# Differential attention: the score products of two heads issued as one group

## The chip, the cores and the metric

The kernel runs on one core of a Trainium2 chip. Its time is the device time of one launch in microseconds (us). Three runs of the kernel before gave 1320.67, 1320.77 and 1320.94 us, so the median is 1320.77 us. Beside the runs there is one profiled execution, from which every duration below is taken.

The engines have short names. PE is TensorE, the matrix engine, and PEld is its weight load, which runs beside the matmuls. DVE is VectorE, ACT is ScalarE, POOL is GpSimd and SP is SyncE, which issues nearly all transfers here. Every engine works through its own queue in order.

## The reference, cut to what matters

The program is a two-layer block for 256 tokens plus 16 learned "meta" tokens, with 1024 features. Each layer has a mixer with three branches (retention, a gated recurrence called hgrn2, and differential attention), a gated sum of the branches, and a feed-forward part with a short convolution. The change touches only the differential attention:

```python
q = rope(q.reshape(b, l, 2 * DA_HEADS, DA_DH), pos).reshape(b, l, DA_HEADS, 2, DA_DH) * DA_DH ** -0.5
k = rope(k.reshape(b, l, 2 * DA_HEADS, DA_DH), pos).reshape(b, l, DA_HEADS, 2, DA_DH)
...
s = jnp.einsum('bqhmd,bkhmd->bhmqk', qb, k)
p = jax.nn.softmax(jnp.where(allowed, s, MASK_VALUE), axis=-1)
w = p[:, :, 0] - lam * p[:, :, 1]
return jnp.einsum('bhqk,bkhe->bqhe', w, v)
...
o = _rms(o) * subln_g.astype(F32) * (1.0 - lambda_init)
```

There are 8 heads. Each head has two maps (m = 0 and 1) of 64 features each. Both maps give a causal softmax over the keys, the second is taken from the first with a learned factor, and the difference weighs 128-wide values. The result of a head is normalised over its 128 features.

## The kernel before, in words

**The main stream.** All dense layers are products of 128 x 128 weight tiles with 272 columns of tokens (258 in the second layer). Each is done as three products of rounded parts (weights high and low, tokens high and low): lines L890, L891 and L892. The weights arrive from memory in chunks of eight tiles (`wraw`, 512 KB). ACT rounds a chunk (`whi`, L575) and DVE makes the remainder (`wlo`, L575). Line L575 is a helper that records every ACT, DVE, POOL and small PE operation, so such operations are told apart by the names of their tiles.

**The rest.** The branches' own small products, softmaxes and norms are placed between main products. No engine has a fixed loop: the program first records every operation with an estimated cost, a key (the time when it should run) and its data, and a planner then simulates the engines and writes out one order for each queue. An operation is not placed more than 12 us (`EARLY`) ahead of its key. An operation that is ready and whose key is overdue goes ahead of a main product. The planner also counts buffers: an operation that opens a new tile is placed only when a buffer of that ring is free in the simulation. The function `behind` records a job (a list of operations), and `settle` spreads the keys of the jobs that end at one mark over the time up to that mark. With `apart` = 2, the first operation of a job waits for the end of the job two places before it: the third head of a block waits for the end of the first.

**The attention.** The heads come in two blocks of four, `+daa` and `+dab`, in each of the two layers, so 16 heads in all. A block is a job `da_first` (the 16 meta queries of its four heads), four jobs `da_head`, and a job `da_tail` (the last 16 tokens). Its result, `da`, is split into rounded parts `b2hi` and `b2lo`, which are the token operands of the main products named `b2`.

**One head.** `da_head` does this, with the names of the tiles:

1. POOL copies 16 columns into `a1` (tag `wts`).
2. PE forms the scores in one recorded operation, `scores` (line L1316): two tiles of keys (272 and 144 wide) times two maps, four calls. A call in 32-bit floats becomes two instructions, so a head has a group of 8. A map takes 64 of the 128 rows of the array. The results go to two banks of PSUM, tag `bank` (name `ds`).
3. DVE adds the mask and takes the row maximum, four times (to `two_a` and `two_b`).
4. ACT exponentiates four times. DVE forms the reciprocals and combines the two maps, in six more instructions.
5. PE transposes three 128 x 128 pieces into `wt` (tag `bank`), ACT copies them to `a1`, POOL copies the tails to `dt`.
6. PE multiplies with the values into `do` (tag `acc`), four instructions.
7. ACT copies two small pieces to `dot`. `sub_norm` squares (`hsq`), rounds (`hsh`, `hsl`), averages on PE (`ms`, tag `bank`), takes the inverse root on ACT (`hr`) and writes `da` on DVE, reading `do` once more.

PSUM has eight banks: four for the main products (two pairs, tag `main`), two with tag `bank` and two with tag `acc`. The tags `wts`, `two_a`, `two_b` and `dm` have two buffers each.

Of the kernel before, what the change touches and what calls it, by code (L numbers as in the profile page):

```python
# [37 lines left out]
TAIL = T - 2 * P  # L38
# [189 lines left out]
C_COS_R, C_SIN_R, C_COS_D, C_SIN_D, C_MASK, C_IDENT, C_OWN, C_DECT, C_FIRST, C_SUM, C_MAP, C_END = \  # L228
# [405 lines left out]
def _trace(ctx, tc, plan, a, depth, probe):  # L634
    nc = tc.nc
    act = _Engine(plan, nc.scalar, "act", 0.094, 0.833e-3)
# [33 lines left out]
    def temp(cols, tag, bufs=2):  # L670
        return new(tp, [P, cols], F32, tag, bufs, tag)
# [16 lines left out]
    def ts(out, x, s1, s2, op0, op1=ALU.bypass):  # L688
        dve.tensor_scalar(out=out, in0=x, scalar1=s1, scalar2=s2, op0=op0, op1=op1)
# [275 lines left out]
    for li in range(depth):  # L965
# [330 lines left out]
            act.activation(st[f"dw{b}"], wt[:, : 4 * META], AF.Copy)  # L1296
            st[f"dt{b}"], st[f"do{b}"] = (temp(P, n, 1).rearrange("p (g h t) -> p g h t", g=2, h=4) for n in ("dt", "dot"))

        def da_head(b, hd):
            q, k, vt, out = st[f"dq{b}"], st[f"dk{b}"], st[f"dvt{b}"], st[f"da{b}"]  # L1300
            scale = DA_DH ** -0.5

            a1 = temp(T + P + TAIL, "wts")
            pool.tensor_copy(a1[:, :META], st[f"dw{b}"][:, hd * META : (hd + 1) * META])
            tiles = ((META + P, T, 0), (META, META + P, T))
            sb = [temp(2 * T, tag) for tag in ("two_a", "two_b")]
            ss = [bank("ds") for _ in range(2)]
            red = temp(12, "dm")
            nm, sm, cf = (red[:, 4 * i : 4 * i + 4].rearrange("p (t m) -> p t m", m=2) for i in range(3))


            def scores():
                for q0, nk, at in tiles:
                    for m in range(2):
                        half = slice(64 * m, 64 * m + 64)
                        nc.tensor.matmul(ss[m][:, at : at + nk], q[half, hd, q0 : q0 + P], k[half, hd, :nk], start=True, stop=True)  # L1316

            plan.add("pe", scores, 0.95, [x[:, : T + P + META] for x in ss], [q[:, hd, :], k[:, hd, :]])
            plan.hold(*sb, a1)
            for i, (q0, nk, at) in enumerate(tiles):  # L1320
                mask = const[:, C_MASK + T - nk : C_MASK + T]
                for m in range(2):
                    cols = slice(at, at + nk)
                    dve.tensor_tensor_reduce(out=sb[m][:, cols], in0=ss[m][:, cols], in1=mask, scale=1.0,
                                             scalar=-3e38, op0=ADD, op1=ALU.max, accum_out=nm[:, i, m : m + 1])
            ts(nm, nm, -scale, None, MUL)
            for i, (q0, nk, at) in enumerate(tiles):
                for m in range(2):
                    p = sb[m][:, at : at + nk]
                    act.activation(p, p, AF.Exp, bias=nm[:, i, m : m + 1], scale=scale, accum_out=sm[:, i, m : m + 1])  # L1330
            dve.reciprocal(cf, sm)
            tt(cf[:, :, 1], cf[:, :, 1], nlam[:, li : li + 1].to_broadcast([P, 2]), MUL)
            for i, (q0, nk, at) in enumerate(tiles):
                p0, p1 = (x[:, at : at + nk] for x in sb)
                ts(p1, p1, cf[:, i, 1:2], None, MUL)
                stt(p0, p0, cf[:, i, 0:1], p1, MUL, ADD)
            w = sb[0]
            wt = bank("wt")
            pe.transpose(wt[:, :P], w[:, :P], ident)
            pe.transpose(wt[:, P : 2 * P], w[:, P : 2 * P], ident)  # L1340
            pe.transpose(wt[:, 2 * P : 3 * P], w[:, T : T + P], ident)
            act.activation(a1[:, META + P : T + P], wt[:, : 2 * P], AF.Copy)
            act.activation(a1[:, META : META + P], wt[:, 2 * P : 3 * P], AF.Copy)

            for g, c in ((0, 2 * P), (1, T + P)):
                pool.tensor_copy(st[f"dt{b}"][:, g, hd, :], w[:, c : c + TAIL])
            o = acc_bank("do")
            ec = slice(hd * P, hd * P + P)
            pe.matmul(o[:, t0:T], vt[:, 0, ec], a1[:, t0:T], start=True, stop=False)
            pe.matmul(o[:, P + META : T], vt[:, 1, ec], a1[:, T : T + P], start=False, stop=True)  # L1350
            for g, c in ((0, 2 * P), (1, P)):
                act.activation(st[f"do{b}"][:, g, hd, :], o[:, c : c + TAIL], AF.Copy)
            sub_norm(out[:, hd, t0 : 2 * P], o[:, t0 : 2 * P])
# [302 lines left out]
```

## Time and profile before

| | before |
|---|---|
| median of three runs | 1320.77 us |
| the profiled execution, its own time | 1320.99 us |
| its span, first to last instruction | 1319.2 us |
| PE, busy share of the span | 99% |
| DVE, ACT, POOL, busy share | 74%, 64%, 6% |
| granted clock of TensorE | 0.999 of full speed |
| score groups of 8 instructions (`ds`, L1316) | 16, first at 285.9 us, last at 1051.9 us |

The profile page gives the busy time of each engine, the chain of work that ended last, and the costliest groups of instructions. The start of one PE instruction to the start of the next is the useful measure on PE, because matmuls overlap in the pipeline: a main product is listed as 0.29 us long, while the next one starts after 0.12 us. In the timelines a row shows the start, the length, the engine, the line, the operation and the names of the tiles, and x8 means that eight instructions of one kind are merged into the row. A wait is put down to the operation that ended last before the waiting one could start.

### The profile page before, as it was taken

What the parts mean: (1) busy time and instruction counts of PE and PEld (TensorE: products, weight loads), DVE (VectorE), ACT (ScalarE), POOL (GpSimd) and SP (SyncE); (2) the same over time, 40 slices, a digit from 0 to 9 for tenths busy, and PEclk for the clock granted to TensorE, in tenths of its full rate; (3) what the DMA queues carried; (4) which work ended last, traced back from release to release, by engine and by line L of the source; (5) the groups of instructions that cost most, each with busy time, mean ns of one, the idle gap of its engine ahead of it and who ended that gap; (6) DMA issues with size and microseconds to landing.
All of it is one profiled execution on the core that took longest, in us unless ns stands there. A gap on an engine that the chain in (4) does not pass through costs nothing.

```text
span 1319.2 us, 27895 instructions
## 1 busy us (share of the span) xinstructions
PE 1311.0 (99%) x11350; PEld 1285.3 (97%) x11350; DVE 970.5 (74%) x1666; ACT 838.5 (64%) x1418; POOL 84.8 (6%) x161
## 2 busy tenths in 40 slices
PE   9999999999999999999999999999999999999998
PEld 9999999999999999999999999999999999999986
DVE  7685797697586789786564857876985867898753
ACT  6757464756576577776456574647565776777743
POOL 5000000000110020000030000100011100200000
PEclk9999999999999999999999999999999999999999
DMA  7654544444544555555555455444445446465653
GB/s 275 192 158 150 170 140 150 135 144 134 184 133 156 178 163 187 176 176 176 176 176 178 150 169 165 146 157 144 145 144 176 142 156 202 157 201 187 204 178 110
DMA packets 60751, 219.03 MB, mean 166 GB/s; under 512 B 6864, under 2 KB 6992, under 8 KB 60624
## 3 DMA queue, kind: packets, MB, share of 16 engines
q1 hardware_dynamic: 60336, 216.74, 51.6%
q8 instruction: 89, 1.46, 0.5%
q10 hardware_dynamic: 288, 0.52, 0.1%
q14 instruction: 38, 0.31, 0.1%
HBM read 216.19 MB, written 1.05 MB: 165 GB/s over the span
## 4 chain that ended last, share of the span: by engine, by line
PE 98%; issue 1%; DMA 1%; SPq 0%; POOL 0%; DVE 0%; ACT 0%; DVEq 0%; POOLq 0%
PE main L890 29%; PE main L892 28%; PE main L891 28%; PE fo L1451 2%; PE fo L1453 2%; PE fo L1452 2%; PE lev L1075 1%; PE ds L1316 1%; PE ms L575 1%; PE do L575 1%; PE ro L575 1%; PE ho L575 1%; PE vt L575 1%; DMA wraw<-in_w 1%; PE wt L575 0%
## 5 line engine op out<-in xcount | busy, mean ns | idle before, releaser
L890 PE MATMUL main<-xh,whi 128*128 128x272 f32 (+1 forms) x2368 | 692.4, 292 | 0.0
L892 PE MATMUL main<-xh,wlo 128*128 128x272 f32 (+1 forms) x2368 | 680.5, 287 | 0.6 <-DVE wlo L575 0.5
L891 PE MATMUL main<-xl,whi 128*128 128x272 f32 (+1 forms) x2368 | 671.4, 284 | 0.0
L575 DVE TENSOR_TENSOR wlo<-wraw,whi 128x1024 fp32r<-128x1024 f32 (+1 forms) x408 | 498.3, 1227 | 224.1 <-ACT whi L575 223.2
L575 ACT ACTIVATE whi<-wraw 128x1024 fp32r<-128x1024 f32 (+1 forms) x408 | 426.5, 1047 | 213.7 <-PE main L891 153.4
L891 PEld LDWEIGHTS main<-xl,whi 128*128 128x128 f32 x2368 | 449.0, 190 | 0.5
L890 PEld LDWEIGHTS main<-xh,whi 128*128 128x128 f32 x2368 | 445.6, 188 | 1.5
L892 PEld LDWEIGHTS main<-xh,wlo 128*128 128x128 f32 x2368 | 444.5, 188 | 1.5 <-DVE wlo L575 1.5
L575 DVE SCALAR_TENSOR_TENSOR two_b<-u,small,two_b 128x256 f32<-128x256 f32 (+2 forms) x176 | 81.4, 504 | 0.9 <-ACT two_b L575 0.7
L575 POOL TENSOR_TENSOR y<-h,rstd 128x272 f32<-128x272 f32 x32 | 36.5, 1175 | 313.6 <-ACT rstd L575 313.6
L575 ACT ACTIVATE two_b<-u,small 128x272 f32<-128x272 f32 (+1 forms) x88 | 49.9, 597 | 4.2 <-DVE u L575 2.5
L892 PE MATMUL main<-ghi,wlo 128*128 128x272 f32 x176 | 51.0, 290 | 0.0
L890 PE MATMUL main<-ghi,whi 128*128 128x272 f32 x176 | 50.9, 289 | 0.0
L891 PE MATMUL main<-glo,whi 128*128 128x272 f32 x176 | 50.2, 285 | 0.0
L575 ACT ACTIVATE u<-main 128x544 f32<-128x544 f32 (+1 forms) x36 | 22.1, 615 | 35.5 <-PE main L892 35.5
L890 PE MATMUL main<-b0hi,whi 128*128 128x272 f32 (+1 forms) x128 | 38.2, 299 | 0.0
L890 PE MATMUL main<-b1hi,whi 128*128 128x272 f32 (+1 forms) x128 | 38.2, 298 | 0.0
L575 POOL COPY tails<-vsrc 128x32 f32<-128x32 f32 x32 | 11.1, 361 | 415.0 <-ACT vsrc L575 364.1
L892 PE MATMUL main<-yhi,wlo 128*128 128x272 f32 (+1 forms) x128 | 36.7, 286 | 0.0
L892 PE MATMUL main<-b2hi,wlo 128*128 128x272 f32 (+1 forms) x128 | 36.6, 286 | 0.0
L892 PE MATMUL main<-b1hi,wlo 128*128 128x272 f32 (+1 forms) x128 | 36.6, 286 | 0.0
L892 PE MATMUL main<-b0hi,wlo 128*128 128x272 f32 (+1 forms) x128 | 36.5, 286 | 0.0
(246 smaller groups left out, 1955.5 us busy)
## 6 DMA issues: line engine op xcount, KB each, us to landing
wraw<-in_w SPq DMA_DIRECT2D x402, 512.0 KB, 3.6
h<-in_h SPq DMA_DIRECT2D x4, 272.0 KB, 5.0
dec<-in_dec SPq DMA_DIRECT2D x2, 544.0 KB, 5.0
wraw<-in_w SPq DMA_DIRECT2D x4, 256.0 KB, 4.7
const<-in_const SPq DMA_DIRECT2D x1, 937.0 KB, 5.6
gain<-in_gl SPq DMA_DIRECT2D x1, 512.0 KB, 5.4
out<-y ACTq DMA_DIRECT2D x2, 256.0 KB, 2.8
out<-y SPq DMA_DIRECT2D x2, 256.0 KB, 2.8
```

The costliest lines, as they stand in the source:

```text
L575: self.plan.add(self.name, lambda: f(*args, **kw), cost, outs, ins, args[2] if method == "activation" else None)
L890: nc.tensor.matmul(o, wh, hi, start=first, stop=False)
L891: nc.tensor.matmul(o, wh, lo, start=False, stop=False)
L892: nc.tensor.matmul(o, wl, hi, start=False, stop=last)
L1075: nc.tensor.matmul(o, keys, x, start=True, stop=True)
L1316: nc.tensor.matmul(ss[m][:, at : at + nk], q[half, hd, q0 : q0 + P], k[half, hd, :nk], start=True, stop=True)
L1451: nc.tensor.matmul(o, gh, wh, start=False, stop=False)
L1452: nc.tensor.matmul(o, gl, wh, start=False, stop=False)
L1453: nc.tensor.matmul(o, gh, wl, start=False, stop=end)
```

## The change

`da_head` becomes `da_heads` and takes two heads. The score calls of both heads are one recorded operation, 8 calls and so 16 instructions, with an estimated cost of 1.8 in place of two times 0.95. The first head's scores go to the two `bank` buffers as before, the second head's to the two `acc` buffers. The operation holds both pairs of `two_a` and `two_b` and both `wts` tiles. The rest is recorded by stages: the row maxima of both heads; then for each head the exponentials and the combination; then for each head the transposes and the copies; then for each head the product with the values and the norm. A block now has four jobs (first, two pairs, tail) in place of six. The number of buffers of every ring stays as it is.

```diff
-        def da_head(b, hd):
+        def da_heads(b, heads):
...
-            a1 = temp(T + P + TAIL, "wts")
-            pool.tensor_copy(a1[:, :META], st[f"dw{b}"][:, hd * META : (hd + 1) * META])
+            a1s = [temp(T + P + TAIL, "wts") for _ in heads]
             tiles = ((META + P, T, 0), (META, META + P, T))
-            sb = [temp(2 * T, tag) for tag in ("two_a", "two_b")]
-            ss = [bank("ds") for _ in range(2)]
-            red = temp(12, "dm")
+            sbs = [[temp(2 * T, tag) for tag in ("two_a", "two_b")] for _ in heads]
+            sss = [[new_bank("ds") for _ in range(2)] for new_bank in (bank, acc_bank)]
...
+            for a1, hd in zip(a1s, heads):
+                pool.tensor_copy(a1[:, :META], st[f"dw{b}"][:, hd * META : (hd + 1) * META])
             def scores():
-                for q0, nk, at in tiles:
+                for ss, hd in zip(sss, heads):
+                    for q0, nk, at in tiles:
+                        for m in range(2):
+                            half = slice(64 * m, 64 * m + 64)
+                            nc.tensor.matmul(ss[m][:, at : at + nk], q[half, hd, q0 : q0 + P], k[half, hd, :nk], start=True, stop=True)
+
+            plan.add("pe", scores, 1.8, [x[:, : T + P + META] for ss in sss for x in ss], [q[:, heads[0] : heads[-1] + 1, :], k[:, heads[0] : heads[-1] + 1, :]])
+            plan.hold(*sum(sbs, []), *a1s)
+            for ss, sb, (nm, _, _) in zip(sss, sbs, stats):
+                for i, (q0, nk, at) in enumerate(tiles):
...
+                        dve.tensor_tensor_reduce(out=sb[m][:, cols], in0=ss[m][:, cols], in1=mask, scale=1.0,
+                                                 scalar=-3e38, op0=ADD, op1=ALU.max, accum_out=nm[:, i, m : m + 1])
+                ts(nm, nm, -scale, None, MUL)
+            for sb, (nm, sm, cf) in zip(sbs, stats):
...
+                        act.activation(p, p, AF.Exp, bias=nm[:, i, m : m + 1], scale=scale, accum_out=sm[:, i, m : m + 1])
+                dve.reciprocal(cf, sm)
...
+            for a1, sb, hd in zip(a1s, sbs, heads):
+                w = sb[0]
+                wt = bank("wt")
+                pe.transpose(wt[:, :P], w[:, :P], ident)
...
+            for a1, hd in zip(a1s, heads):
+                o = acc_bank("do")
...
+                sub_norm(out[:, hd, t0 : 2 * P], o[:, t0 : 2 * P])
...
-                for hd in range(4):
-                    behind(lambda: da_head(b, hd), "da", 2)
+                for hd in (0, 2):
+                    behind(lambda: da_heads(b, (hd, hd + 1)), "da", 2)
```

More of the change, by code (lines that the diff above doesn't have):

```diff
@@ L1318, in da_head @@
[L1318 to L1353, printed above, removed]
+            sbs = [[temp(2 * T, tag) for tag in ("two_a", "two_b")] for _ in heads]
@@ new lines, in da_heads @@
+            sss = [[new_bank("ds") for _ in range(2)] for new_bank in (bank, acc_bank)]
+            stats = []
+            for _ in heads:
+                red = temp(12, "dm")
+                stats.append([red[:, 4 * i : 4 * i + 4].rearrange("p (t m) -> p t m", m=2) for i in range(3)])
+            for a1, hd in zip(a1s, heads):
+                pool.tensor_copy(a1[:, :META], st[f"dw{b}"][:, hd * META : (hd + 1) * META])
+            def scores():
+                for ss, hd in zip(sss, heads):
[3 more added lines that the diff above has]
+                            nc.tensor.matmul(ss[m][:, at : at + nk], q[half, hd, q0 : q0 + P], k[half, hd, :nk], start=True, stop=True)
@@ new lines, in da_heads @@
+            for sb, (nm, sm, cf) in zip(sbs, stats):
+                for i, (q0, nk, at) in enumerate(tiles):
+                    for m in range(2):
+                        p = sb[m][:, at : at + nk]
+                        act.activation(p, p, AF.Exp, bias=nm[:, i, m : m + 1], scale=scale, accum_out=sm[:, i, m : m + 1])
+                dve.reciprocal(cf, sm)
+                tt(cf[:, :, 1], cf[:, :, 1], nlam[:, li : li + 1].to_broadcast([P, 2]), MUL)
+                for i, (q0, nk, at) in enumerate(tiles):
+                    p0, p1 = (x[:, at : at + nk] for x in sb)
+                    ts(p1, p1, cf[:, i, 1:2], None, MUL)
+                    stt(p0, p0, cf[:, i, 0:1], p1, MUL, ADD)
@@ new lines, in da_heads @@
+            for a1, hd in zip(a1s, heads):
+                o = acc_bank("do")
+                ec = slice(hd * P, hd * P + P)
+                pe.matmul(o[:, t0:T], vt[:, 0, ec], a1[:, t0:T], start=True, stop=False)
+                pe.matmul(o[:, P + META : T], vt[:, 1, ec], a1[:, T : T + P], start=False, stop=True)
+                for g, c in ((0, 2 * P), (1, P)):
+                    act.activation(st[f"do{b}"][:, g, hd, :], o[:, c : c + TAIL], AF.Copy)
+                sub_norm(out[:, hd, t0 : 2 * P], o[:, t0 : 2 * P])
```

11 lines of the change are left out of this document (8 added, 3 removed).

## The prediction

> **What bounds the kernel now.** I read the page first, for the busy shares and the shares of the chain that ended last.
>
> ```profile
> span 1319.2 us, 27895 instructions
> PE 1311.0 (99%) x11350; PEld 1285.3 (97%) x11350; DVE 970.5 (74%) x1666; ACT 838.5 (64%) x1418; POOL 84.8 (6%) x161
> PE 98%; issue 1%; DMA 1%; SPq 0%; POOL 0%; DVE 0%; ACT 0%; DVEq 0%; POOLq 0%
> ```
>
> PE is busy 99% of the span and is 98% of the chain. A busy PE may still be waiting inside a modelled matmul, so the second view is the list of waits of PE over the whole run. It has three rows.
>
> ```profile
> PE warm L575 <- POOL ones_d L575: 1.0, 1, 1.0
> PE main L892 <- DVE wlo L575: 0.5, 3, 0.2
> PE vm L575 <- POOL tails L575: 0.4, 1, 0.4
> ```
>
> Only 0.9 us of waiting lies behind the start, and none of it is on a score or on a bank of PSUM. So the time is the length of PE's queue: an edit gains what it takes out of that queue, and loses what it makes PE wait. The third view is the chain around the scores.
>
> ```profile
> 285.93 0.91 PE ds L1316 x8
> 286.84 0.32 PE main L890
> ...
> 1051.91 0.90 PE ds L1316 x8
> ```
>
> The chain has 16 such rows of 0.90 or 0.91 us, one per head. After a group the first main product takes 0.32 us in it. What a group really costs is read from PE's timeline.
>
> ```profile
> 285.02 0.29 PE L890 MATMUL main<-b0hi,whi 128*128 128x272 f32 x1
> ...
> 285.64 0.29 PE L892 MATMUL main<-b0hi,wlo 128*128 128x272 f32 x1
> 285.86 0.97 PE L1316 MATMUL ds<-dk,dq 64*128 64x272 f32 x8
> 286.77 0.39 PE L890 MATMUL main<-b0hi,whi 128*128 128x272 f32 x1
> 287.00 0.29 PE L891 MATMUL main<-b0lo,whi 128*128 128x272 f32 x1
> ```
>
> Between the first two rows lie five starts in 0.62 us: a main product goes by every 0.124 us. From the last main product before the group to the second one after it are 287.00 - 285.64 = 1.36 us, where two steps of 0.124 would stand without the group. The group costs 1.36 - 0.25 = 1.11 us. Narrow windows on the same group show its inner starts; a row merges what its window meets and begins with the first of them.
>
> ```profile
> 285.87 0.72 PE L1316 MATMUL ds<-dk,dq 64*128 64x272 f32 x3
> ...
> 286.20 0.64 PE L1316 MATMUL ds<-dk,dq 64*128 64x272 f32 x5
> ...
> 286.43 0.41 PE L1316 MATMUL ds<-dk,dq 64*128 64x144 f32 x3
> ...
> 286.55 0.29 PE L1316 MATMUL ds<-dk,dq 64*128 64x144 f32 x2
> ```
>
> The eight instructions go in four pairs, one of each map, each on its own half of the rows. Pair to pair: 0.33, 0.23 (both 272 wide), 0.12 (144 wide), and then 286.77 - 286.55 = 0.22 to the main product, though that last pair is also 144 wide. The bare stream is therefore 0.23 + 0.23 + 0.12 + 0.12 = 0.70 us, and the other 0.40 is paid for going into the group and out of it: 0.22 - 0.124 = 0.10 before it, 0.33 - 0.23 = 0.10 in its first pair, 0.22 - 0.12 = 0.10 after its last, and 0.23 - 0.124 = 0.10 on the second main product.
>
> **The change, part by part.**
>
> *One group for two heads.* 16 groups become 8. The work of 16 stays, and so do the 0.40 us of 8 of them. The step that no trace of before shows is the seam, from the last pair of the first head to the first pair of the second. If it is like the other inner steps it costs 0.12, and a group of 16 costs 0.40 + 2 x 0.70 = 1.80 us. If the array starts afresh there, 0.10 after a last pair and 0.10 in a first pair come back, and 0.20 is saved in place of 0.40. More than 0.40 can't be saved, since the streams stay. I take the full 0.40: within a group the array already goes on to another tile of queries and from 272 to 144 columns without a mark in the starts, and the seam asks for no more. Sum: 8 x 0.40 = 3.2 us, the lower end 8 x 0.20 = 1.6.
>
> The Trainium skill has a price for part of this: "TensorE: Matmul & The Clock Gate", section "LDWEIGHTS (loading the stationary operand)", gives a load of 128 columns as 128 / 1.2 = 107 ns. An estimate from that page, with one load exposed at the entry and one at the exit, is 0.21 us a group and 1.7 us in all, where the rows have four marks of 0.10. The skill's "TensorEngine Tiling (Array Packing)", "Key Properties", adds that a change of tiling mode drains the engine, which fits the rows better than two loads.
>
> *Groups that had no main product behind them.* Three of the 16 groups run straight into a product with the values. I looked whether these already save something that the change can't save again.
>
> ```profile
> 315.75 0.29 PE L892 MATMUL main<-xh,wlo 128*128 128x272 f32 x1
> 315.97 0.97 PE L1316 MATMUL ds<-dk,dq 64*128 64x272 f32 x8
> 316.87 0.95 PE L575 MATMUL do<-wts,vt 128*128 128x272 f32 x4
> ...
> 317.78 0.28 PE L891 MATMUL main<-xl,whi 128*128 128x272 f32 x1
> ...
> 381.04 0.28 PE L892 MATMUL main<-b1hi,wlo 128*128 128x272 f32 x1
> 381.17 0.84 PE L575 MATMUL do<-wts,vt 128*128 128x272 f32 x4
> ...
> 381.98 0.28 PE L891 MATMUL main<-b1lo,whi 128*128 128x272 f32 x1
> ```
>
> Together they cost 317.78 - 315.75 - 0.25 = 1.78 us. Alone, the product costs 381.98 - 381.04 - 0.25 = 0.69, and with a group of 1.11 that is 1.80. So 0.02 us at most: nothing to correct. The same rows say that it matters little how the transposes, products and means are cut up among the main products: four passes cost 0.69 alone, against 0.67 inside. The new order by stages is costed at nothing for that reason, with 0.3 us of play either way.
>
> *DVE, ACT and POOL.* No instruction is added or removed, and no transfer; SP's queue is not touched. What changes is that both heads' maxima become ready at once, so eight maxima and then eight exponentials can stand in a row before the next chunk of weights. The work that hides this is the lead of the weights. Before already had both bursts, in the second block of the first layer.
>
> ```profile
> 373.40 0.52 ACT L575 ACTIVATE two_a<-two_a,dm 128x272 f32<-128x272 f32 x1
> ...
> 377.04 1.99 ACT L575 ACTIVATE whi<-wraw 128x1024 fp32r<-128x1024 f32 x2
> ...
> 369.93 0.43 DVE L575 CUSTOM_DVE_ANT_0 two_a<-ds,const 128x272 f32<-128x272 f32 x1
> ...
> 371.22 0.17 DVE L575 TENSOR_SCALAR dm<-dm 128x4 f32<-128x4 f32 x1
> ```
>
> Eight exponentials held ACT for 377.04 - 373.40 = 3.64 us ahead of a rounding of weights, and PE waited for nothing there. On DVE one head's four maxima take 371.22 + 0.17 - 369.93 = 1.46 us; the second head's, right behind, delay a remainder `wlo` by that much more than before. Cost taken: 0, bounds 0 and 8 x 1.46 = 11.7 us. I take the lower end, because the nearest row, the list of waits, has 0.5 us of such waiting in the whole run. POOL is busy 6%, so the two copies to `a1` side by side cost nothing.
>
> *The wait that is added.* The group needs all four auxiliary banks empty. The two `acc` banks are the new condition: each is held by the product with the values until `sub_norm` has read it for the last time, on DVE.
>
> ```profile
> 385.96 0.48 DVE L575 SCALAR_TENSOR_TENSOR da<-do,subg,hr 128x256 f32<-128x256 f32 x1
> 386.74 1.23 DVE L575 TENSOR_TENSOR wlo<-wraw,whi 128x1024 fp32r<-128x1024 f32 x1 [0.30 <-ACT whi L575]
> 387.88 0.48 DVE L575 SCALAR_TENSOR_TENSOR da<-do,subg,hr 128x256 f32<-128x256 f32 x1
> ```
>
> The second pair of a block can't begin before both reads of the first pair. PE's queue is in order, so if the group stands in it too early, every main product behind it waits too, and after some microseconds the ends of the main products that ACT and DVE wait for. The planner places the group where its own simulation has the banks free, and by the list of waits its placing was never early for a bank. Cost taken: 0; the upper end is the distance of the two reads, 1.92 us, in each of the four blocks, 7.7 us. A gain is excluded, as before has no such wait.
>
> *The end of the attention.* The pairs now follow each other strictly. Its last consumer is the second half of the `b2` products: five tiles of features in, 24 products after the first.
>
> ```profile
> 1071.42 1.23 DVE L575 TENSOR_TENSOR b2lo<-da,b2hi 128x1032 fp32r<-128x1032 f32 x1
> ...
> 1077.61 0.28 PE L890 MATMUL main<-b2hi,whi 128*128 128x258 f32 x1
> ...
> 1080.46 0.28 PE L890 MATMUL main<-b2hi,whi 128*128 128x258 f32 x1
> ```
>
> The remainder is there at 1072.65 and needed at 1080.46, so 7.8 us are free. How long the pairs take is read from the chain's rows of the scores and, for the second layer, the last read of `do`.
>
> ```profile
> 368.26 0.90 PE ds L1316 x8
> ...
> 1021.80 0.90 PE ds L1316 x8
> ...
> 1066.10 0.47 DVE L575 SCALAR_TENSOR_TENSOR da<-do,subg,hr 128x242 f32<-128x242 f32 x1 [0.17 <-ACT hr L575]
> ```
>
> In the first layer's second block one pair took 388.36 - 368.26 = 20.1 us, up to the second read shown above. Two such pairs in a row are 40, where the four heads of the second layer's second block took 1066.57 - 1021.80 = 44.8. The strict order costs nothing that is seen.
>
> *Sum.* Span 1319.2 - 3.2 = 1316.0. The profiled execution took 1320.99 us, 1.8 more than its span and 0.2 more than the median of 1320.77. Against the median: 1317.6 us, 0.24% less.
>
> **The rivals.**
>
> *The seam starts afresh.* The array pays 0.20 at each seam, as worked out above: 1.6 us less, 1319.2 us. For it speaks that banks and operands of another head begin there; against it the smooth inner steps.
>
> *The weights come late.* DVE's second run of four maxima delays a remainder, and PE waits at L892. Where the lead is gone this costs 1.46 us. The group lands in eight places; at two of them it would be 2.9 us, which eats the gain: 1320.5. For it speaks that DVE is the busiest engine behind PE and that PE waited for `wlo` three times before; against it that this was 0.5 us in all.
>
> *PE stands before a bank.* This is the one on the slower side. In each block's second pair the group reaches the head of PE's queue when one `acc` bank is read out and the other is not: 4 x 1.92 = 7.7 us of waiting, 1320.8 - 3.2 + 7.7 = 1325.3 us. It decides from 3.2 + 2.6 = 5.8 us on, or 1.45 us a block. For it speaks that four banks must be free at once and that the last readers stand in DVE's queue behind pieces of weights of 1.23 us; against it the empty list of waits of before. The skill warns in the same direction: "TensorEngine Tiling (Array Packing)", "Gotcha 1: PSUM Pressure", says that row tiling raises the pressure on PSUM and that the software must see to the order. No run here has shown that yet.
>
> **How the numbers follow.** A difference under about 0.2%, 2.6 us, can't be told from none in this kernel. The forecast, 3.2 us less with no new wait, gets 0.52; its own range is 1316.6 to 1318.1 (the 0.3 of play, and up to half a microsecond of small waits). The fresh start gets 0.09 and the late weights 0.15; both end within 0.2%, 0.24 together. The wait for a bank gets 0.24, more than the list of waits alone would give, because an order that the planner makes anew has not been seen. That makes faster 0.52, same 0.24, slower 0.24. The range of all cases is 1316.4 to 1325.0: it takes in the first three, and a third of the last.
>
> **What would show it.** Right: eight rows of 16 instructions of about 1.6 us (0.90 + 0.70) in the chain, a step of 0.12 at the seam, the main products' 0.124 unchanged, and PE's list of waits still under 1 us behind the start. Wrong: a step of 0.3 at the seam; rows of PE waiting for `wlo`; rows of `ds` waiting for DVE's last read of `do`; `b2` products waiting for `b2lo`, if the pairs take more than 20 us each. The prediction also falls if PE's queue is cut up worse elsewhere, as the planner reorders all that follows.

## The result, and the profile after

The changed kernel takes 1318.63 us (median of 22 runs, 1317.9 to 1319.45). The kernel before, on the same chip, takes 1320.84 us (22 runs, 1320.12 to 1321.79). The ratio is 0.9983, with a 95% interval from 0.9977 to 0.999: 2.2 us less, where 3.2 were forecast. That is inside the range of all cases, and 0.5 us above the forecast's own range, whose upper end was 1318.1.

The page of the kernel after has the same shape: the span, the busy time of the engines, and the shares of the chain that ended last.

```profile
span 1317.4 us, 27905 instructions
PE 1308.3 (99%) x11350; PEld 1284.2 (97%) x11350; DVE 970.5 (74%) x1666; ACT 839.6 (64%) x1418; POOL 84.7 (6%) x161
PE 98%; DVE 1%; ACT 0%; DMA 0%; SPq 0%; issue 0%; POOL 0%
```

PE's busy time fell by 2.7 us at the same 11350 instructions. The list of waits of PE, after (total, times, longest):

```profile
PE warm L575 <- POOL ones_d L575: 1.0, 1, 1.0
PE main L890 <- ACT whi L575: 0.7, 1, 0.7
PE main L892 <- DVE wlo L575: 0.6, 3, 0.2
PE wt L575 <- POOL dt L575: 0.2, 1, 0.2
```

There is no row for the scores and none for a bank. Behind the start stand 1.5 us, against 0.9 in the profile before. The prediction's sign of being right was under 1 us, so this one failed. The 0.7 for `whi` stands ahead of the first main product, at 6 us, and differs from one execution to the next: a second profile of the unchanged kernel before has 0.4 there, where the first had none. The row for `dt` is in both profiles of the kernel after and in neither of the kernel before; it comes back below.

The chain of the kernel after has eight rows for the scores, all of 1.61 us; these are its first and its last.

```profile
292.37 1.61 PE ds L1321 x16
...
1043.23 1.61 PE ds L1321 x16
```

The timeline of PE around the last group (start, length, then the instruction), with narrow windows inside it. As before, a row starts with the first instruction that its window meets.

```profile
1042.95 0.28 PE L892 MATMUL main<-b1hi,wlo 128*128 128x258 f32 x1
1043.16 1.68 PE L1321 MATMUL ds<-dk,dq 64*128 64x272 f32 x16
...
1043.72 0.64 PE L1321 MATMUL ds<-dk,dq 64*128 64x144 f32 x6
...
1043.84 0.52 PE L1321 MATMUL ds<-dk,dq 64*128 64x144 f32 x4
...
1043.96 0.40 PE L1321 MATMUL ds<-dk,dq 64*128 64x272 f32 x2
...
1044.76 0.39 PE L890 MATMUL main<-b1hi,whi 128*128 128x258 f32 x1
1044.99 0.28 PE L891 MATMUL main<-b1lo,whi 128*128 128x258 f32 x1
```

The first head's last pair of products starts at 1043.84, the second head's first pair at 1043.96: the seam is a step of 0.12 us, the cheap one. The whole group costs 1044.99 - 1042.95 = 2.04, less two plain steps of 0.12, or 1.80 us, as forecast. So the groups did what was said, and the missing microsecond is elsewhere.

To find it, the steps from one PE start to the next were added up between the same two main products in a repeated profile of each kernel (the runs before_again and after_again below). A piece of short work costs the time from the last main product ahead of it to the second one behind it, less the plain steps that would stand there without it, of 0.1244 us at 272 columns and 0.1197 at 258. Where a score group runs straight into a product with the values, that product is taken off at the price that it has alone, 0.685 or 0.66 us. In us, after less before:

```
main products                   1700 to 2900   6500 to 8000     sum
score groups                           -1.60          -1.55   -3.15
other short products                   -0.01          +0.58   +0.57
plain steps between mains              -0.04          +0.56   +0.52
all                                    -1.65          -0.41   -2.07
```

The groups are worth 3.15 us. Before, 13 of the 16 cost 1.09 to 1.11 us each, and the three that run straight into a product with the values come to 1.10 when that product is taken off. The eight of the kernel after cost 1.80 to 1.82.

The 0.57 us of the other short products are lost at two places of the second layer, one in each block, where the transpose of the tails (`wt` from `dt`) comes to the head of PE's queue before POOL has copied the last tail. These are DVE's work, POOL's copy and PE's rows at the larger one, in the kernel after.

```profile
1054.01 1.22 DVE L575 TENSOR_TENSOR wlo<-wraw,whi 128x1024 fp32r<-128x1024 f32 x1
```

```profile
1054.16 1.13 POOL L575 COPY dt<-two_a 128x16 f32<-128x16 f32 x1 [0.41 <-DVE two_a L575]
```

```profile
1054.51 0.60 PE L575 MATMUL do<-wts,vt 128*128 128x258 f32 x2
1055.34 0.33 PE L575 MATMUL wt<-const,dt 128*128 128x128 f32 x1 [0.23 <-POOL dt L575]
1055.51 0.39 PE L575 MATMUL do<-wts,vt 128*128 128x128 f32 x2
```

The copy takes 1.13 us, where the median of the 32 copies to `dt` is 0.20. It starts while DVE works on a `wlo` and ends 0.06 us behind that, and so do all the long ones: in this trace 15 of the 64 copies to `dt` and to `tails` took over 0.3 us, and each ended 0.05 to 0.07 us behind a DVE operation on two tiles (TENSOR_TENSOR) beside which it had begun. PE starts the transpose 0.05 us after the copy's end and 0.61 us after the product ahead of it; the step to a transpose is 0.11 where nothing holds it up. The piece costs 1.33 us, and its six instructions cost 0.88 elsewhere: 0.45 us lost, of which the list of waits shows 0.2, because it counts from the modelled end of the product. The other place, at 980.31 us, loses 0.15 and is not in the list.

The last 0.52 us are in the main products themselves. These windows of 31 us in the second layer show it: PE's own work in the kernel before, then in the kernel after.

```profile
1072.00:1103.00 31.00, 31.00 (x264) 1.00 0.57 185
```

```profile
1072.00:1103.00 31.00, 31.00 (x261) 1.00 0.57 177
```

Nothing but main products runs there, at a granted clock of 1.00 in both, and in the same time the kernel before gets three more through. Taken from the starts, it had a stretch from about main product 7640 to 7958 with a step of 118.1 ns; the kernel after has 119.7 there, as both have nearly everywhere else for products of 258 columns.

### The profile page after: what moved, and what is told of

Its sections match the earlier page's. It is cut to its first block, busy times and chain, and to the rows that moved or that the text cites. A ratio compares the mean times of both kernels' runs of the same rounds, so it can differ in the third digit from the quotient of the medians.

```text
span 1317.4 us, 27905 instructions
## 1 busy us (share of the span) xinstructions
PE 1308.3 (99%) x11350; PEld 1284.2 (97%) x11350; DVE 970.5 (74%) x1666; ACT 839.6 (64%) x1418; POOL 84.7 (6%) x161
## 4 chain that ended last, share of the span: by engine, by line
PE 98%; DVE 1%; ACT 0%; DMA 0%; SPq 0%; issue 0%; POOL 0%
PE main L892 29%; PE main L890 29%; PE main L891 28%; PE fo L1460 2%; PE fo L1462 2%; PE fo L1461 2%; PE lev L1075 1%; PE ds L1321 1%; PE ms L575 1%; PE ro L575 1%; PE ho L575 1%; PE do L575 1%; PE vt L575 1%; PE s L575 0%; PE wt L575 0%; DMA h<-in_h 0%
```

## The experiments

All times are medians; each comparison is with runs of the kernel before on the same chip, at 1320.6 to 1320.95 us.

### Both kernels once more

No edit.

> The kernel before, unchanged, for a second profile. The forecast was 3.2 us less, the measured medians differ by 2.2. One theory: the missing microsecond is partly a property of the old order. In the old profile the main products of the second layer from about 1067 to 1104 us go by every 118.1 ns, in the profile after the same products every 119.7, which is 0.5 us over 300 products. If that is a property of the order, this second profile shows the same stretch at the same products. The rival: it belongs to one execution, and this profile shows 119.7 there. Time 1320.8 in both cases.

> The changed kernel, unchanged, for a second profile. If the difference of 0.46 us at the start (the first main product at 6.05 us in the profile after, at 5.80 before, and 0.2 more in the first 30 products) is chance, the start moves again by some tenths of a microsecond between these two profiles, and attention saves the same amount. Time 1318.6; no faster stretch from 1067 to 1104 us if that belongs to the old order.

Before: 1320.85 us (ratio 1.0002, 0.9993 to 1.0011). After: 1318.4 us (0.9983, 0.9974 to 0.9992). Between the two profiles of the kernel after, the rows of the table agree to 0.02 us. The two of the kernel before differ in one thing, 0.43 us of standing before a transpose (`vm`) in the first and not in the second. The start does move: main product 100 begins at 21.03 and at 20.11 us in the two profiles of the kernel after. The quick stretch is in both profiles of before and in none of after, so it belongs to the order of the instructions, not to chance. (Some of the expectations below speak of a third layer. The program has two, and the second is meant.)

### The seam opened

```diff
                 for ss, hd in zip(sss, heads):
+                    if hd != heads[0]:
+                        nc.tensor.matmul(ss[0][:, 416:512], ones_h, ones_h[:, :96], start=True, stop=True)
                     for q0, nk, at in tiles:
```

> The changed kernel with one product on all 128 rows (96 columns, 0.04 us of stream, its result is not used) between the two heads' scores, inside the same recorded operation, so every queue keeps its order. Theory, going into and out of the half-row products costs 0.40 us and that is the whole gain: the cost comes back eight times, plus 8 x 0.04: +3.5 us against the changed kernel, about 1322.1, and the group's rows show marks of 0.1 around the inserted product. Rival, the gain comes from the new order of the rest: only the inserted products count, +0.3 to +0.8 us, about 1319.2.

Measured 1322.43 us, 4.0 above the repeated kernel after (ratio to before 1.0011, 1.0002 to 1.002). Its timeline of PE at the last group:

```profile
1046.02 0.28 PE L892 MATMUL main<-b1hi,wlo 128*128 128x258 f32 x1
1046.22 0.97 PE L1323 MATMUL ds<-dk,dq 64*128 64x272 f32 x8
1047.13 0.31 PE L1319 MATMUL ds<-ones_h 128*128 128x96 f32 x1
1047.37 0.97 PE L1323 MATMUL ds<-dk,dq 64*128 64x272 f32 x8
1048.27 0.39 PE L890 MATMUL main<-b1hi,whi 128*128 128x258 f32 x1
1048.49 0.28 PE L891 MATMUL main<-b1lo,whi 128*128 128x258 f32 x1
```

The group now costs 1048.49 - 1046.02 - 0.24 = 2.23 us, 0.43 more. A product of that size costs 0.11 among main products (the run nudge, below), so leaving the 64-row products and coming back costs about 0.32 of it. The price is for changing between products over half and over all of the rows. It is not one for products of plain 32-bit floats among rounded ones: the products with the values are such products over all rows, and alone they cost 0.68 to 0.69 us at 272 columns, hardly more than the 0.23, 0.23, 0.11 and 0.11 of their own steps. The Trainium skill, "TensorEngine Tiling (Array Packing)", section "Key Properties", says that a change of tiling mode drains the engine; the trace agrees and adds the size.

### Two groups again, the rest by stages

```diff
-            def scores():
-                for ss, hd in zip(sss, heads):
+            parts = []
+            for ss, hd in zip(sss, heads):
+                def scores(ss=ss, hd=hd):
...
-            plan.add("pe", scores, 1.8, ...)
+                parts.append(plan.add("pe", scores, 0.95, ...))
...
+                        if ss is sss[0] and i == m == 0:
+                            plan.queue(parts[1], plan.ops[-1])
```

> The changed kernel with its stages, its four banks and its holds, but the scores of the two heads as two operations, the second placed after the first row maximum of the first head, so that main products stand between them. Theory (0.40 us for each group): 16 groups of 1.1 us again, +3.1 us against the changed kernel, about 1321.7. Rival (the order by stages brings the gain): about 1318.6 as the changed kernel.

Measured 1321.12 us (1.0003, 0.9994 to 1.0012): 2.7 us over after, and level with before. Its starts give 3.2 us more for the score groups, and 0.5 less for the rest: there is no wait for `dt` in this run, and its other short products are within 0.02 us of the kernel before. The quick stretch is missing here too. Joining the groups is the whole gain; the order by stages alone brings none.

### One group, the rest head by head

The group of 16 and its four banks stay; the exponentials, transposes, products and norm of a head are recorded together again.

```diff
-            for ss, sb, (nm, _, _) in zip(sss, sbs, stats):
+            for a1, hd, ss, sb, (nm, sm, cf) in zip(a1s, heads, sss, sbs, stats):
...
-            for sb, (nm, sm, cf) in zip(sbs, stats):
...
-            for a1, sb, hd in zip(a1s, sbs, heads):
...
-            for a1, hd in zip(a1s, heads):
```

> The 16 products of two heads in one group and their four banks as in the kernel after, but everything behind the scores recorded head by head again, not by stages. Theory (the eight groups carry the whole gain, the order by stages only moves other short products about): eight groups of about 1.81 us, the transposes and the second main products cut up as in the kernel before or close to it, 1317.6 to 1318.6 us. If the order by stages is what gave back 0.9 us of the forecast 3.2, it should come out at 1317.6; if the four banks or the place of the groups did, at the 1318.4 of the kernel after. A stretch of main products at 118.2 ns in place of 119.7, as the kernel before has it in the third layer, would show by itself in the steps between main products, and is worth 0.5 us.

Measured 1319.67 us (0.999, 0.9981 to 0.9998), 1.0 to 1.3 over the kernel after, and above all that was expected. Its list of waits has a row that the kernel after lacks.

```profile
PE vm L575 <- POOL tails L575: 1.2, 2, 0.9
```

PE stands for two transposes of the values' tails. The long quick stretch didn't come back either. For the next run GpSimd's second copy of the tails was planned dearer, which puts those transposes some twelve main products later.

```diff
                         pool.tensor_copy(tails[:, 1], src[:, :, P : P + TAIL])
+                        plan.ops[-1].cost += 1.4
```

> As the run with the scores grouped and the rest recorded head by head, with GpSimd's second copy of the values' tails planned 1.4 us dearer, which puts the transpose of those tails (vm) some twelve main products later in the two layers. In the trace of that run the tensor engine stood 1.2 us before vm, for copies that took 1.2 us where others of the same shape take 0.2. Theory (that stand is all that run has over the kernel after, and the order by stages is worth some tenths against it): no wait before vm, 1318.1 us (1317.5 to 1318.7), at or a few tenths below the kernel after's 1318.5. Rival (what the head by head order saves is spent elsewhere, or the moved products cost what the stand did): 1319.2 us or more.

Measured 1318.08 us (0.998, 0.9971 to 0.9988). The row for `vm` is gone; these are all of its waits:

```profile
PE warm L575 <- POOL ones_d L575: 1.0, 1, 1.0
PE main L892 <- DVE wlo L575: 0.4, 2, 0.2
```

Against the repeated kernel after, the starts give 0.69 us less over the two stretches, all of it in the other short products; 0.6 of it are the two transposes of the tails, which no longer stand. In the median it is 0.3 to 0.6 us, which the intervals can't tell from nothing. The order by stages need not cost this, as the run with two groups has that order without the stand. What costs is a transpose that comes too soon behind POOL's copies. This is shown by the starts, not by the times.

### The bank read late

The last read of `do` for the second head of each first pair is issued eleven times, with the order on all engines as it was. It writes the same values each time.

```diff
                 sub_norm(out[:, hd, t0 : 2 * P], o[:, t0 : 2 * P])
+                if hd == 1:
+                    last = plan.ops[-1]
+                    last.run = lambda run=last.run: [run() for _ in range(11)]
```

> The kernel after with the last read of the second main product of the first pair of heads carried out eleven times in a row by the vector engine, at an unchanged order on every engine. Ten more reads of 0.48 us put the last read 4.8 us later. In the traces of the kernel after, the tenth product of the following group, the first to write into that bank, starts 1.88, 2.27, 2.62 and 2.10 us after the read ends, in the four places. Theory (the bank is released by the last read, and the tensor engine stands until then): waits of 2.9, 2.5, 2.2 and 2.7 us in front of the tenth product of the second groups, 10.3 us together, so 1328.7 us (1327.5 to 1330). Rival (later reads are hidden, the group doesn't wait for them): 1318.4 us within 0.5. Rival (the vector engine's delay reaches the halves of the weights instead): waits on wlo of more than 1 us.

Measured 1339.2 us: 20.7 over the kernel after, twice what was expected. The waits came near the forecast of 10.3 us:

```profile
PE ds L1321 <- DVE da L575: 9.8, 4, 2.9
```

Much of the other 11 us is seen in windows around the first stand (busy time and count of PE, PEld, DVE, ACT and POOL, then the granted clock, the DMA share and GB/s).

```profile
306.00:312.00 6.00, 6.00 (x51) 5.78 (x51) 4.49 (x9) 3.91 (x7) 0.00 (x0) 1.00 0.54 182
312.50:315.50 3.00, 0.34 (x2) 0.00 (x0) 2.82 (x7) 0.00 (x0) 0.00 (x0) 0.95 0.00 0
316.00:322.00 6.00, 6.00 (x26) 5.52 (x25) 5.35 (x23) 3.12 (x10) 0.00 (x0) 0.50 0.29 89
322.00:328.00 6.00, 6.00 (x51) 6.00 (x50) 4.58 (x14) 3.94 (x12) 0.79 (x4) 1.00 0.27 93
```

Behind a stand of 3 us the granted clock is at one half for 6 us, and PE gets 26 products through where it got 51. From the starts, main products go by every 227 ns until 322.0. Each of the other three stands is followed by 3.4 us at half the clock, which begin up to 1.4 us after PE has gone on. This window is behind the shortest of them, a wait of 1.97 us that ended at 982.83.

```profile
984.21:987.62 3.41, 3.41 (x17) 3.41 (x17) 3.28 (x20) 1.44 (x3) 0.00 (x0) 0.50 0.45 154
```

So PE pays for a stand twice. By the starts the four interrupted groups cost 20.0 us more, of which 9.8 are waits. The next run shows a further 0.7 us at each place without a slower clock, so 2.7 of the rest; that leaves some 7.5 us for the half clock. The next run makes the stands shorter, with eight reads in place of eleven.

```diff
-                    last.run = lambda run=last.run: [run() for _ in range(11)]
+                    last.run = lambda run=last.run: [run() for _ in range(8)]
```

> The run with late reads of the bank, with seven more reads in place of ten, so the last read comes 3.4 us later in place of 4.8. With ten, the tensor engine's steps before the group's tenth product were 3.25, 2.86, 2.36 and 2.88 us, the waits 9.8 us together, and the products behind three to four of the four stands ran at half the clock for 1.1 to 6.3 us more, which cost as much again: 1339.2 us. Theory (a stand of less than some 2 us leaves the clock alone): steps of 1.8, 1.4, 0.9 and 1.4 us, waits of 4.1 us, the granted clock at 1.00 throughout, 1322.5 us (1321.8 to 1323.2). Rival (any stand of a microsecond halves the clock): 1325 us or more, with main products at 227 ns behind the stands.

Measured 1327.38 us, above the 1322.5 of the theory. Its two largest waits behind the start, and windows around its first stand:

```profile
PE ds L1321 <- DVE da L575: 3.6, 4, 1.3
...
PE wt L575 <- DVE two_a L575: 0.7, 2, 0.6
```

```profile
312.00:314.00 2.00, 0.74 (x6) 0.70 (x6) 1.93 (x4) 0.00 (x0) 0.00 (x0) 1.00 0.00 0
314.00:316.00 2.00, 2.00 (x17) 1.88 (x15) 1.97 (x13) 0.94 (x1) 0.00 (x0) 1.00 0.37 82
316.00:318.00 2.00, 2.00 (x19) 2.00 (x18) 1.97 (x11) 2.00 (x10) 0.00 (x0) 1.00 0.47 180
```

The clock stays at 1.00, as the theory said. If the length of the wait decides, the limit lies between the longest wait of this run and the shortest of the run before it; in the timelines they stand in front of the last six products of a group.

```profile
313.26 0.94 PE L1321 MATMUL ds<-dk,dq 64*128 64x272 f32 x6 [1.29 <-DVE da L575]
```

```profile
982.83 0.94 PE L1321 MATMUL ds<-dk,dq 64*128 64x272 f32 x6 [1.97 <-DVE da L575]
```

But the time was missed by 5 us. The starts put 1.1 to 2.0 us to each interrupted group, 6.4 in all against 3.6 of waits: 0.7 us more per place (0.68 to 0.71). That it is the second entry into the group is not shown; at the opened seam leaving and coming back cost half of that, 0.32. Another 1.9 us are transposes that came late behind the delayed vector engine. The Trainium skill, "TensorE: Matmul & The Clock Gate", section "Why this matters for your kernels", asks for no gap above about 3 us; here a wait of 1.97 us already brought the half clock.

### The quick rhythm

Is the step of 118.1 ns a state of the stream, or does it belong to what else happens then? One product of 96 columns, into unused columns, was put into the kernel before ahead of main product 7824, in the middle of its quick stretch.

```diff
+            nudge = [whole[i][:, f, 300:396]] if not begun and len(plan.main) >= 2600 and not nudged else []
+            nudged.extend(nudge)
...
+                for x in nudge:
+                    nc.tensor.matmul(x, ones_h, ones_h[:, :96], start=True, stop=True)
                 nc.tensor.matmul(o, wh, hi, start=first, stop=False)
```

> The kernel before with one more product of 96 columns in the middle of the stretch that ran at the quick rhythm, ahead of main product 7824 (the stretch went from 7632 to 7968); nobody reads it. Theory (the quick rhythm is a state of the stream that lasts until something breaks it): main products at 118.2 ns up to 7824 and at 119.7 behind it, 144 of them, so 0.2 us more and 0.05 for the product itself, 1321.1 us. Rival (the quick rhythm belongs to what else happens at that time, the transfers or the data): 118.2 ns goes on behind the product to 7968.

Measured 1321.38 us (1.0004, 0.9995 to 1.0013). By its starts the products go by every 118.1 ns up to the inserted one and every 119.7 right behind it. It is a state of the stream, and here one short product ends it.

The opposite was tried in the kernel after: 22 such products of 16 to 100 columns, one ahead of each pair of the stage `fi` (the first products of the feed-forward part) in the second layer.

```diff
...
+            nudge = [whole[i][:, f, 300 : 316 + 4 * j]] if li == 1 and name == "fi" and f == 0 and not begun else []
```

> The kernel after with one more product ahead of each of the 22 pairs of the stage fi in the third layer, of 16, 20, 24 and so on to 100 columns, into unused columns of the pair's bank; nobody reads it. It asks whether the quick rhythm of the main products (118.2 ns for one of 258 columns, in the kernel before over 336 products in this stage; 119.7 elsewhere) is a state that a break of the right length in the stream sets off. Theory: yes; then some of the 22 stretches of 48 products run at about 118 ns and the others at 119.7, and the time is that of the kernel after, plus 22 products of 0.03 to 0.07 us, less up to 0.07 us for each quick stretch: 1318.3 to 1319.9 us. Rival: the rhythm has nothing to do with breaks in the stream; all stretches run at 119.7 ns and the time is 1319.1 to 1319.9 us.

Measured 1321.39 us (1.0005, 0.9996 to 1.0014), 2.8 to 3.0 over the kernel after. Behind none of the 22 did the quick rhythm set in; in one stretch it came later, behind two short products of the stage itself, and the next inserted product ended it. Each inserted product cost 0.108 to 0.116 us, whatever its width; the estimate of 0.03 to 0.07 from the columns was wrong. Then breaks of other shapes, in a single run:

```diff
...
+            widths = ((128,), (160,), (192,), (208,), (224,), (240,), (240, 128), (240, 64), (128, 128), (64, 64), (16, 16),
+                      (240, 240), (128, 16), (16, 128), (16,) * 3, (16,) * 4, (16,) * 5, (16,) * 6, (64,) * 3, (128,) * 3,
+                      (240,) * 3, (16,) * 8)
+            nudge = [whole[i][:, f, 272 : 272 + w] for w in widths[j]] if li == 1 and name == "fi" and f == 0 and not begun else []
```

> One look, for the quick rhythm alone: the 22 single products of up to 100 columns set off no quick stretch, each cost 0.11 us whatever its width. Here the 22 breaks in the stage fi of the third layer are of one product (128 to 240 columns), of two (240 and 128 down to 16 and 16) and of three to eight. Nobody reads them. Theory (breaks of the right length set the quick rhythm off): some of the 22 stretches at about 118 ns. Rival (they don't): all at 119.7. The time is worth nothing here: 57 more products at about 0.11 us, some 6 us over the kernel after, 1325 us.

It took 1324.14 us. The mean step from the starts behind each break, once it had settled:

```
quick, 118.0 to 118.1 ns:  192; 208; 224; 64+64; 240+240; 3 x 16; 4 x 16; 3 x 240; 8 x 16
plain, 119.6 to 119.8 ns:  128; 240; 240+128; 240+64; 128+128; 16+16; 128+16; 16+128;
                           5 x 16; 6 x 16; 3 x 64; 3 x 128
left out:                  160 (the stage's own short products fall into its stretch)
```

Nine of the breaks are followed by the quick rhythm, with no order in their widths. Four of them (64+64, 240+240, 3 x 16, 3 x 240) came on a plain stream and set it off; the other five came on a quick one and kept it. In the last run the pair of 64 columns was put into the run with `vm` later, at two places.

```diff
+            if fresh and (li == 1 and (name, j) == ("fi", 2) or len(plan.main) >= 2584 and not nudged):
+                nudge = [whole[i][:, f, 272:336]] * 2
+            nudged.extend(nudge)
...
+                for x in nudge:
+                    nc.tensor.matmul(x, ones_h, hi[:, :64], start=True, stop=True)
```

> As the run with vm later, with two products of 64 columns into unused columns put in front of a pair of the main products at two places of the third layer, where no other short product follows for some time: ahead of main product 7776 and of 8208 (of 9168). Nobody reads them. In the look at wide breaks a pair of 64 columns cost 0.23 us and was followed by main products at 118.1 ns, in place of 119.75. Theory (such a break sets the quick rhythm off wherever it stands in a steady stream): 118.1 ns from 7776 to 8160 and from 8208 to 9168, which saves 384 and 960 times 1.65 ns, 2.2 us, less 0.46 for the four products: 1316.3 us (1315.6 to 1317.0), below both kernels. If the second place alone sets it off, 1317.0; if neither, 1318.5. Rival (what the step does there hangs on the phase in which the break meets the stream): one or none of the two.

Measured 1316.6 us (0.9967, 0.9955 to 0.9979), 4.2 less than before, 1.5 less than without the four products, and below both kernels. These windows of PE's main products are of this run and then of the run with `vm` later.

```profile
1140.00:1240.00 100.00, 100.00 (x850) 1.00 0.58 196
```

```profile
1140.00:1240.00 100.00, 100.00 (x838) 1.00 0.58 192
```

Twelve more main products in 100 us: 847 would be 100 / 0.1181, 835 are 100 / 0.1197, and each count has two or three more that overlap the edges. Behind the second place the rhythm held to the end, 960 products. Behind the first it held from 7776 to 7958 or so and then fell back with nothing inserted there, at the product at which it had ended in the kernel before.

## Why the prediction was right, and where it fell short

*One group for two heads.* Right. The eight rows of 16, the 1.61 us in the chain, the seam of 0.12 and the 1.80 us per group are all as written. Over all groups 3.15 us were saved, where 3.2 were forecast, and the three groups without a main product behind them needed no correction, as was said. The rival of a fresh start at the seam is refuted by the step of 0.12, and opening the seam cost 0.43.

*The order by stages, "costed at nothing", with 0.3 us of play.* This is the term that was mis-sized. The other short products moved by +0.57 us. The main products, of which the prediction wrote "the main products' 0.124 unchanged", lost 0.52, as the new order doesn't pass into the quick rhythm that the old one had for some 320 products. Together 1.1 us, in place of 0.3 at most. The prediction's last sentence, on a queue cut up worse elsewhere, named this and gave it no price. The quick stretch stood in the trace of before, in its starts from 1072 to 1103 us, and was not looked at: the step between main products was read at one place and taken for all.

*DVE, ACT and POOL.* Right for DVE and ACT: waits for `wlo` are 0.6 us, against 0.5 before, and the rival of late weights is refuted. Wrong for POOL. The prediction took its busy share of 6% as a reason that its copies cost nothing, and looked at the copies to `a1` alone. The copies of the tails, to `dt`, held PE up at two places, for 0.45 and 0.15 us, which is all of the 0.57 above. In the order head by head PE stood 1.2 us for two others of POOL's copies.

*The wait that is added.* Costed at 0, rightly. The last read of `do` ahead of the last group, on DVE:

```profile
1041.41 0.47 DVE L575 SCALAR_TENSOR_TENSOR da<-do,subg,hr 128x242 f32<-128x242 f32 x1
```

It ends at 1041.88, 1.28 us before the group's first product at 1043.16. But the rival was priced wrongly. It took 7.7 us of standing for 7.7 us of time; in the run with late reads 9.8 us of waiting made 20.7. Waits of 1.92 us lie near the 1.97 that was followed by half the clock, and waits of 1.29 already cost 0.7 more than their length, so 7.7 would have been a lower end. And the point from which it decides, 5.8 us of standing, was too high: in the run with eight reads, the four interrupted groups cost 2.8 us over their waits.

*The end of the attention.* Right. The remainder for the second half of `b2`, on DVE, and the first `b2` product, on PE:

```profile
1068.95 1.23 DVE L575 TENSOR_TENSOR b2lo<-da,b2hi 128x1032 fp32r<-128x1032 f32 x1
```

```profile
1075.26 0.28 PE L890 MATMUL main<-b2hi,whi 128*128 128x258 f32 x1
```

It is ready at 1070.18; the product that needs it comes 24 products, 2.9 us, after 1075.26. The slack is 8 us, where 7.8 were found before.

*The sum.* -3.2 forecast. -3.15 from the groups, +0.57 from the short products that stand for POOL and +0.52 from the rhythm make -2.1, and the medians say -2.2 and -2.5. So the gain's mechanism and size were right, and two losses were left out. That the measured time fell inside the range of all cases owes something to luck: the room above the forecast's own range had been given for a fresh start at the seam, for late weights and for a wait before a bank, and none of the three came.

## What to carry to other kernels

Where one engine's queue is the whole time, price an edit by the steps from start to start, over the whole stretch that gets a new order, and not at one place: 1.3% of a step of 120 ns, over 320 products, was a sixth of the forecast gain. A small busy share doesn't make an engine free: one copy on POOL, busy 6%, took 1.13 us beside DVE's work in place of 0.20 and cost 0.45 us, because its reader came too soon. Put products over half of the rows together; going into such a group and out of it again cost some 0.4 us here. And price a stand of TensorE by more than its length: in this kernel each stand inside a group cost 0.7 us on top, and waits of 1.97 us and more were followed by half the clock for 3.4 us or longer.

## What the runs showed of the hardware that was not expected

The stream of products of 258 columns has two rhythms, 118.1 and 119.7 ns, at the same granted clock. A break sets the one or the other, reproducibly for one order, and mostly the next break ends it; it also fell back at main product 7958 or so with no break, in the kernel before and in the last run, some 40 products after the stage's input changes. What decides it is open: neither the width nor the number of the inserted products orders the results.

A short product costs 0.11 us among main products whether it has 16 or 100 columns, nearly the step of a product of 258.

Four waits of TensorE, of 1.97 to 2.86 us, were followed by half the granted clock, for 3.4 us three times and for 6.8 us with the longest, there from 0.5 us before its end. In two places the clock fell only 1.4 us after the wait was over. Four waits of 0.46 to 1.29 us were not followed by it. Where between 1.29 and 1.97 us the limit lies, and whether it is the same in every place, was not tried.

GpSimd's copies to `dt`, all of one shape, took 0.20 us in the median and up to 1.28 in the kernel after. The long ones ended right behind a DVE operation on two tiles, in 15 cases of 15, so by the trace such a copy stands for DVE; no run moved the one against the other. Whether PE stands behind it differs from order to order.
